# Modulation sums moved within a hybrid mLSTM / gated-delta-rule block, and a quarter of the feed-forward input scaled by GpSimd

## The chip, the cores and the metric

The kernel runs on one core of one Trainium2 chip. Five engines of the core matter here: TensorE (PE in the profile) multiplies matrices, VectorE (DVE), ScalarE (ACT) and GpSimd (POOL) work on elements, and SyncE (SP) issues most of the large loads. Each takes its own instructions in the order in which the program lists them. The metric is the device time of one launch in microseconds: the median of the runs of a kernel.

## The reference

One transformer-like layer on 256 tokens of width 2048, in fp32:

- `mod = silu(c) @ W_ada + b_ada`, cut into six rows of 2048: shift, scale and gate for the mixer and for the feed-forward part. In the kernel each 128 of its 12288 columns is one sum over a row of 2048 products: these are the **modulation sums**.
- `h = RMSNorm(x)*(1+scale_m)+shift_m`, then one input projection of `h`, whose columns feed an mLSTM branch (4 heads), a **gated delta rule** branch (16 heads of 128, chunks of 64, both directions) and two merge gates.
- Per chunk the delta rule needs the inverse of a unit-triangular 64x64 matrix, then `u = T(beta v)`, `w = T(beta e^g k)`, and a scan `S = a S + k^T v_new`; the output is normed per head and gated.
- Both branches are projected, merged and projected out ("o"), `x = x + gate_m * out`.
- `hf = RMSNorm(x)*(1+scale_f)+shift_f`, `x = x + gate_f * ((silu(hf W_gate) * (hf W_up)) W_down)`, and a last RMSNorm.

## The kernel before, in words

Weights arrive as fp32, 1 MB at a time on SP's queue (`raw`, 4 buffers). ScalarE rounds a half of such a piece to `wh` (L171, L197), VectorE makes the remainder `wl` (L172, L198), each with 3 buffers, and TensorE runs three passes: `wh` by the high and the low part of the activations, `wl` by the high part. A job of 4 pieces for two token tiles is `tjob` (L182-245; matmuls of 128x512 at L215, L216, L218), a job for a column block with the tokens as columns is `fjob` (L162-180; 128x256 at L175, L177). `acc_<job>` names the accumulators.

The **delta rule** goes in four groups g of four heads, each in two pairs p of two heads. Between groups the inverse of the blocks is begun on VectorE (`gdn_invert`, 30 steps of two operations at L663 and L669 on the tile `uu`), stored to memory by GpSimd (L655), read back in another layout as `cg` (L682), transposed and mixed into `R` (L684-689). Then `gdn_phase2` (L707-804) is a chain of short steps in which each engine waits for the other: `p1` (TensorE, L717) to `pt0` (VectorE, L718) to `p2` (L726) to `Et` and `X` (VectorE L729, ScalarE L730-733) to `p3` (L739) to `pt1` (L740) to `p4` (L751) to `UL` (L752, L753) to `pa` (L763, L764) to `z` (L767, L768) to `pb` (L775) to `r` (L776) to `pc` to `z` to `po` (L785-790) to a norm (`gdn_norm`, L805-822: squares on ScalarE at L809, a square root at L813, reciprocal L814, four scalings on VectorE at L819) to `px` (L796) and out (L798). The jobs of the other projections stand between these steps as **filler**: `stream` and `fill` put pieces of jobs there, by the tables `after` and `last`.

The **modulation sums** are one generator per part of 2048 columns (`ada_part`, L120-131). One sum is a 1 MB load on SP's queue and one VectorE operation on 128x2048 (L127), with the buffers of `raw` or, later, of the tile `ada`. Parts 2, 3 and 4 (48 sums) belong to the mixer's gate and the feed-forward's shift and scale; part 5 (16 sums) to the last gate. `sums(n)` runs the next n of them, and `pump()`, which every job calls after each of its pieces, runs one on each `every[0]`-th call; zero stops it. The output projection "o" has four quarters g (512 columns each), and calls `sums()` at the steps that a table names. After its last quarter come the residual (L1113, L1114), the token's norm (L1123-1125), the feed-forward input scaled by the norm (`normed`, into `xn`, L1191 or L1193), its transpose (`pxn`, L1200), scale and shift into `hf` (L1204 or L1206), the high and low parts (L1207, L1210), and the first gate job.

The order in which the instructions stand on each engine isn't the order of the Python text alone: the kernel is built with a scheduler that simulates the engines' time lines (`schedule_with_timeline_sim=True`), and places each operation where its simulation has it ready. Only operations inside `order(...)` keep the text's order among themselves. So an edit in one place can move rows in many.

Of the kernel before, what the change touches and what calls it, by code (L numbers as in the profile page):

```python
# [12 lines left out]
ALU = mybir.AluOpType  # L13
# [39 lines left out]
def hybrid_block(ctx: ExitStack, tc: tile.TileContext, xr, nfr, crow, pk_d, cst_d, ada2, ada4, win0, winb, wint, wba, wbb, wo, wgu, wd, out, dbg=None):  # L53
    nc = tc.nc
    V, S, G, PE = nc.vector, nc.scalar, nc.gpsimd, nc.tensor

    def pool(stack, name, bufs=1, **kw):
        return stack.enter_context(tc.tile_pool(name=name, bufs=bufs, **kw))
# [27 lines left out]
    def order(ins, yes=True):  # L86

        return tc.keep_in_program_order(ins) if yes else ins
# [58 lines left out]
    count, every = [0], [0]  # L147
# [97 lines left out]
    def run(job):  # L245
        for _ in job:
            pass
# [3 lines left out]
    def fill(n=1):  # L251

        while n and fills:
            if next(fills[0], None):
                n -= 1
            else:
                fills.pop(0)
# [633 lines left out]
    for g in range(4):  # L891
        if g == 3:
            sf.close()
            op = pool(so, "op", side="right")
        blocks = gdn_blocks(g)
        next(blocks)
        fill(8)
        next(blocks)
        fill(1)
        pairs = [gdn_phase2(g, p) for p in range(2)]  # L900
        every[0] = (0, 2, 2, 2)[g]
        for p in range(2):
            pieces = stream(4 * g + 2 * p + 4)
            if g == 3:
                o4s += [o_load(i, op, 3) for i in ((0, 1), (2,))[p]]
            for n in range(1, 10):
                next(pairs[p], None)
                if p == 0:
                    next(blocks, None)
                for _ in range(after[n] if g < 3 else last[n]):  # L910
                    next(pieces)
            for _ in pairs[p]:
                pass

            if g < 3:
                while 4 * g + 2 * p + 5 not in heads:
                    next(pieces)
        if g < 3:
            fills.insert(0, z_job(g + 1))
            every[0] = 0  # L920
            invert(g + 1)
# [166 lines left out]
    mgh, mgl = big(bigC, F32R, "mgh"), big(bigC, F32R, "mgl")  # L1088
    for g in range(4):
        if g == 3:  # L1090
            every[0] = 0
            while len(background) > 2:
                sums()
            row_store(2, ml, 0.5)
        run(y_a(g, mgh, mgl))
# [32 lines left out]
    rs1 = xp.tile([P, 3], F32, name="rs1")  # L1128
# [23 lines left out]
    for g in range(4):  # L1152
        def done_o(*a, g=g):
            for t, ps in [a] if g == 3 else enumerate(a[0]):
                residual(t, g, ps, gm, ss1, wp, g == 3)
                if g == 3:
                    token_rstd(ss1, rs1, t)

        if g == 3:
            root()  # L1160
        between = (lambda: next(gt0)) if g == 3 else None
        for i, _ in enumerate(tjob(f"o{g}", [wo[g, u] for u in range(4)], mgh, mgl, done_o, by_token=between)):
            if i in ((4, 6, 7), (1, 2, 4, 6), (1, 2, 4, 6), (1, 2, 4))[g]:
                sums()
            if g == 3 and i == 4:
                sums(P)
                V.scalar_tensor_tensor(
                    affn, mod[:, 4 * KB : 5 * KB], 1.0, pk[:, PK_NFFN : PK_NFFN + KB], ALU.add, ALU.mult
                )
# [16 lines left out]
    def normed(q, t, parts, eng):  # L1186
        if q not in xns:
            xns[q] = hp.tile([P, 2, 512], F32, tag="sg", bufs=2, name=f"xn{q}")
        o, i = xns[q][:, t, parts], x1[:, t, q * 512 + parts.start : q * 512 + parts.stop]
        if eng is V:  # L1190
            order(V.tensor_scalar(o, i, rs1[:, t : t + 1], None, ALU.mult))  # L1191
        else:
            order(S.activation(o, i, AF.Copy, scale=rs1[:, t : t + 1]))  # L1193

    def moved(b):

        px = gps(f"pxn{b}")
        for t in range(2):
            f = b % 4 * P
            order(PE.transpose(px[:, t * P : (t + 1) * P], xns[b // 4][:, t, f : f + P], ident))  # L1200
        hfs[b] = hp.tile([P, T], F32, tag="hf", bufs=2, name=f"hf{b}")
        f, m = affn[:, b : b + 1], mod[:, 3 * KB + b : 3 * KB + b + 1]
        if b % 2 and b > 2:
            order(S.activation(hfs[b], px[:, 0:T], AF.Identity, scale=f, bias=m))  # L1204
        else:
            order(V.tensor_scalar(hfs[b], px[:, 0:T], f, m, ALU.mult, ALU.add))  # L1206
        order(S.activation(hfh[:, b], hfs[b], AF.Copy))  # L1207
# [5 lines left out]
    normed(0, 1, slice(0, 256), V)  # L1213
    for t in range(2):
        normed(0, t, slice(256, 512), S)
    moved(0)
    moved(1)
    low(0)
# [4 lines left out]
    for b in range(2, KB, 2):  # L1223

        next(gt0)
        low(b)
        low(b + 1)
        next(gt0)
        if b % 4 == 2 and b < 12:
            for t in range(2):  # L1230
                normed(b // 4 + 1, t, slice(0, 512), S)
        for e in (b + 2, b + 3):
            if e < KB:
                moved(e)
# [3 lines left out]
    for j in range(FB // 4):  # L1238
# [4 lines left out]
        for e2 in range(2):  # L1243
# [5 lines left out]
            b = 4 * j + 2 * e2  # L1249
# [144 lines left out]
```

## Time and profile before

| what | value |
| --- | --- |
| median of 3 runs (lowest, highest) | 1985.31 us (1982.88, 1988.02) |
| the profiled execution: time, span | 1979.27 us, 1977.3 us |
| its mean granted TensorE clock | 0.988 |
| PE busy | 1918.9 us, 97% of the span |
| DVE / ACT / POOL busy | 1402.5 / 1022.7 / 96.9 us |
| the two chains of delta-rule group 3 | 861.69 to 948.23 us |
| from the last quarter of o into the first gate job | about 1250 to 1290 us |

Times in the trace are microseconds from the start of the span, and they are those of one execution, which took 6.0 us less than the median. A row of a time line gives start, length, engine, line, operation and tiles; what stands in brackets is how long the engine was idle before it and which operation it waited for. Matmul lengths overlap, since they are pipelined.

### The profile page before, as it was taken

To read this page: it belongs to the slowest core of one execution; us is meant where nothing else is said; L and a number is where in the kernel's file an instruction comes from. 1 tells how busy PE (TensorE), PEld (TensorE's weight loads), DVE (VectorE), ACT (ScalarE), POOL (GpSimd) and SP (SyncE) were. 2 spreads that over 40 slices of the span, in tenths; PEclk is the share of its full clock that TensorE was granted. 3 is DMA by queue.
4 is the path that set the end of the run, shared out by engine and by line. 5 is a ranking of instruction groups with operands and counts; after the bars stand their busy time and mean duration, and the time that the engine had idled before them with its cause. 6 is when DMAs were issued, how large, how long until landed. Compare 5 with 4: busy or idle time off the path is not lost.

```text
span 1977.3 us, 27036 instructions
## 1 busy us (share of the span) xinstructions
PE 1918.9 (97%) x10352; PEld 1705.5 (86%) x10352; DVE 1402.5 (71%) x2091; ACT 1022.7 (52%) x1568; POOL 96.9 (5%) x185
## 2 busy tenths in 40 slices
PE   8999999999999999999799999799999999999997
PEld 6887889989989998998688888688888888888886
DVE  5779887878988996965587769766666655555554
ACT  3146657855765686465454444554444444444443
POOL 0000300110100011000200000000000000000000
PEclk9999999999999999999799999899999999999999
DMA  9996665567667765885677679466766765566563
GB/s 400 420 383 194 222 223 192 167 203 283 228 199 247 281 214 191 310 303 190 234 291 266 249 288 419 182 234 235 265 244 237 262 246 193 205 240 203 202 206 114
DMA packets 78675, 487.76 MB, mean 247 GB/s; under 512 B 10265, under 2 KB 15681, under 8 KB 23889
## 3 DMA queue, kind: packets, MB, share of 16 engines
q1 hardware_dynamic: 63360, 450.95, 62.2%
q0 software_dynamic: 7872, 19.99, 4.4%
q10 hardware_dynamic: 7314, 15.10, 2.1%
q8 instruction: 81, 1.33, 0.3%
q14 instruction: 48, 0.39, 0.1%
HBM read 469.16 MB, written 16.83 MB: 246 GB/s over the span
## 4 chain that ended last, share of the span: by engine, by line
PE 73%; DVE 11%; DMA 9%; ACT 4%; issue 2%; POOL 0%; SPq 0%; ACTq 0%; DVEq 0%; POOLq 0%
DMA ra<-ada 5%; PE acc_up L215 4%; PE acc_up L218 4%; PE acc_up L216 4%; PE acc_d L216 4%; PE acc_d L215 4%; PE acc_d L218 4%; PE acc_gt L216 4%; PE acc_gt L215 4%; PE acc_gt L218 4%; PE acc_o L218 2%; PE acc_o L216 2%; PE acc_o L215 2%; PE acc_a L175 2%; PE acc_b L175 2%
## 5 line engine op out<-in xcount | busy, mean ns | idle before, releaser
L198 DVE TENSOR_TENSOR wl_d<-raw_d,wh_d 128x1024 fp32r<-128x1024 f32 x88 | 107.8, 1225 | 102.7 <-ACT wh_d L197 102.7
L127 DVE SCALAR_TENSOR_TENSOR ada<-ada,crow 128x2048 f32<-128x2048 f32 x64 | 146.5, 2289 | 43.6 <-DMA ada<-ada 43.5
L198 DVE TENSOR_TENSOR wl_up<-raw_up,wh_up 128x1024 fp32r<-128x1024 f32 x88 | 107.5, 1225 | 95.9 <-ACT wh_up L197 95.9
L197 ACT ACTIVATE wh_d<-raw_d 128x1024 fp32r<-128x1024 f32 x88 | 93.0, 1057 | 130.5 <-PE acc_d L216 125.3
L198 DVE TENSOR_TENSOR wl_gt<-raw_gt,wh_gt 128x1024 fp32r<-128x1024 f32 x88 | 107.7, 1224 | 72.4 <-ACT wh_gt L197 68.2
L197 ACT ACTIVATE wh_gt<-raw_gt 128x1024 fp32r<-128x1024 f32 x88 | 92.9, 1056 | 120.7 <-PE acc_gt L216 73.2
L197 ACT ACTIVATE wh_up<-raw_up 128x1024 fp32r<-128x1024 f32 x88 | 93.0, 1056 | 118.2 <-PE acc_up L216 71.7
L215 PE MATMUL acc_gt<-wh_gt,hfh 128*128 128x512 f32 x352 | 135.2, 384 | 0.0
L216 PE MATMUL acc_gt<-wh_gt,hfl 128*128 128x512 f32 x352 | 134.6, 382 | 0.0
L175 PE MATMUL acc_b<-hh,wh_b 128*128 128x256 f32 x576 | 134.6, 276 | 0.0
L175 PE MATMUL acc_b<-hl,wh_b 128*128 128x256 f32 x576 | 134.6, 277 | 0.0
L215 PE MATMUL acc_up<-wh_up,hfh 128*128 128x512 f32 x352 | 133.5, 379 | 0.0
L216 PE MATMUL acc_up<-wh_up,hfl 128*128 128x512 f32 x352 | 133.5, 379 | 0.0
L216 PE MATMUL acc_d<-wh_d,ffl 128*128 128x512 f32 x344 | 130.4, 379 | 0.0
L215 PE MATMUL acc_d<-wh_d,ffh 128*128 128x512 f32 x344 | 130.4, 379 | 0.0
L530 PE MATMUL first<-x,raw 128*128 128x256 f32 x512 | 114.5, 382 | 7.5 <-ACT x L523 6.8
L530 PEld LDWEIGHTS first<-x,raw 128*128 128x128 f32 x512 | 96.1, 190 | 25.9 <-ACT x L523 12.4
L175 PEld LDWEIGHTS acc_b<-hl,wh_b 128*128 128x128 f32 x576 | 110.6, 192 | 0.4
L175 PEld LDWEIGHTS acc_b<-hh,wh_b 128*128 128x128 f32 x576 | 110.5, 192 | 0.5
L197 ACT ACTIVATE wh_o<-raw_o 128x1024 fp32r<-128x1024 f32 x64 | 67.1, 1054 | 58.9 <-PE acc_o L216 35.5
L218 PE MATMUL acc_gt<-wl_gt,hfh 128*128 128x512 f32 x352 | 95.3, 385 | 0.0
L171 ACT ACTIVATE wh_b<-raw_b 128x1024 fp32r<-128x1024 f32 x72 | 76.1, 1058 | 37.1 <-PE acc_b L175 22.8
(384 smaller groups left out, 5018.4 us busy)
## 6 DMA issues: line engine op xcount, KB each, us to landing
ada<-ada SPq DMA_DIRECT2D x64, 1024.0 KB, 5.8
raw_gt<-wgu SPq DMA_DIRECT2D x44, 1024.0 KB, 5.0
raw_up<-wgu SPq DMA_DIRECT2D x44, 1024.0 KB, 4.9
raw_d<-wd SPq DMA_DIRECT2D x44, 1024.0 KB, 4.9
raw_b<-winb SPq DMA_DIRECT2D x36, 1024.0 KB, 5.0
ra<-ada SPq DMA_DIRECT2D x32, 1025.0 KB, 15.8
raw<-win SPq DMA_DIRECT2D x16, 1024.0 KB, 17.1
raw_z<-wint SPq DMA_DIRECT2D x16, 1024.0 KB, 5.2
```

Source lines behind the costliest of these rows:

```text
L127: V.scalar_tensor_tensor(raw, raw, 1.0, row_c[:, :D], ALU.mult, ALU.mult, accum_out=mod[:, c0 + b : c0 + b + 1])
L171: S.activation(wh, raw[:, k0 : k0 + 8], AF.Copy)
L175: PE.matmul(o, wh[:, k], both(x, k0 + k).rearrange("p a b -> p b a"), start=k0 + k + i == 0, stop=False)
L197: order(S.activation(wh, raws[u][:, k0 : k0 + 2], AF.Copy), hold)
L198: order(V.tensor_tensor(wl, raws[u][:, k0 : k0 + 2], wh.bitcast(F32), ALU.subtract), hold)
L215: order(PE.matmul(ps[t], tok(xh, kk, t), turns(wh[:, k]), start=kk == 0, stop=False), early and steps > 1)
L216: PE.matmul(ps[t], tok(xl, kk, t), turns(wh[:, k]), start=False, stop=False)
L218: PE.matmul(ps[t], tok(xh, kk, t), turns(wl[:, k]), start=False, stop=kk == last)
L530: PE.matmul(first[o], raw[:, o], x[:, b], start=b == 0 and o % 2 == 0, stop=b == KB - 1 and o % 2 == 1)
```

## The change

Four things, all outside the arithmetic:

1. In the delta rule's group 0, `every[0]` is 3 in place of 0: one modulation sum on each third `pump()` while its two chains and their filler run. Groups 1 to 3 keep 2.
2. Before the last quarter of the mLSTM branch's projection `y_a`, `every[0] = 0` is gone. The value stays 2 from there to the line `every[0] = 4` after the feed-forward input.
3. The table of o's own sums becomes `(4,6,7), (2,4,6), (1,3), ()`: none in its last quarter.
4. The second quarter of the feed-forward input (`normed(1, ...)`) goes to GpSimd, right after the first quarter, and the third and fourth, still on ScalarE, are asked for at blocks 4 and 8 in place of 6 and 10.

```diff
-        every[0] = (0, 2, 2, 2)[g]
+        every[0] = (3, 2, 2, 2)[g]
...
     for g in range(4):
         if g == 3:
-            every[0] = 0
             while len(background) > 2:
                 sums()
...
-            if i in ((4, 6, 7), (1, 2, 4, 6), (1, 2, 4, 6), (1, 2, 4))[g]:
+            if i in ((4, 6, 7), (2, 4, 6), (1, 3), ())[g]:
                 sums()
...
-        if eng is V:
-            order(V.tensor_scalar(o, i, rs1[:, t : t + 1], None, ALU.mult))
+        if eng is not S:
+            order(eng.tensor_scalar(o, i, rs1[:, t : t + 1], None, ALU.mult))
...
+    for t in range(2):
+        normed(1, t, slice(0, 512), G)
...
-        if b % 4 == 2 and b < 12:
+        if b % 4 == 0 and b < 12:
             for t in range(2):
                 normed(b // 4 + 1, t, slice(0, 512), S)
```

One line fewer from L1091 on makes the changed kernel's lines one smaller than before in the residual and the feed-forward input (L1112 there is L1113 here).

Where it moves instructions: first **TensorE in group 3's first chain**. `p_3_0` are the chain's small products, `acc_...` the accumulators of filler jobs (o and a are mLSTM projections, ma a merge gate). Before:

```order
L218 MATMUL acc_o_0_8664<-wl_o_3_2_8856,hh 128x512
L751 MATMUL p_3_0_8333<-X,pt_3_0_8303 128x64 x4
L218 MATMUL acc_o_1_8665<-wl_o_3_2_8856,hh 128x512
...
L175 MATMUL acc_a_0_8875<-hl,wh_a_0_0_8878 128x256
L177 MATMUL acc_a_0_8875<-hh,wl_a_0_0_8879 128x256 x2
L763 MATMUL pa_0_8383<-vv_6624,UL 128x128
L177 MATMUL acc_a_0_8875<-hh,wl_a_0_0_8879 128x256 x6
L764 MATMUL pa_0_8383<-vv_6624,UL 128x128
L763 MATMUL pa_0_8383<-vv_6864,UL 128x128
```

and with the change:

```order
L218 MATMUL acc_ma_0_9193<-wl_ma_3_2_9344,hh 128x512
L218 MATMUL acc_ma_1_9194<-wl_ma_3_2_9344,hh 128x512
L717 MATMUL p_3_0_8237<-R,cc_1107 128x32
L717 MATMUL p_3_0_8237<-R,cc_1108 128x32
...
L726 MATMUL p_3_0_8268<-R,pt_3_0_8238 128x32 x4
L739 MATMUL p_3_0_8320<-X,cc_1107 128x64
L739 MATMUL p_3_0_8320<-X,cc_1108 128x64
...
L751 MATMUL p_3_0_8351<-X,pt_3_0_8321 128x64 x4
L763 MATMUL pa_0_8401<-vv_6640,UL 128x128
L764 MATMUL pa_0_8401<-vv_6640,UL 128x128
```

Before, each step of the chain has matmuls of filler jobs ahead of it and behind it. Now the filler job `ma` ends before `p1` (L717), and from there to the last `px` (L796) of the second pair no row of an `acc_` tile stands on TensorE; the jobs o, a and ma all lie ahead of it.

Second, **VectorE at the same place** (`wl_...` are remainders of filler weights, `ada_...` modulation sums). Before:

```order
L718 TENSOR_TENSOR pt_3_0_8222<-p_3_0_8221,cst 128x512
L198 TENSOR_TENSOR wl_o_2_0_8758<-raw_o_2_8755,wh_o_2_0_8757 128x1024
L198 TENSOR_TENSOR wl_o_2_2_8781<-raw_o_2_8755,wh_o_2_2_8780 128x1024
L729 STREAM_TRANSPOSE Et_0_8257<-p_3_0_8252 128x128
L127 SCALAR_TENSOR_TENSOR ada_5_8934,mod<-ada_5_8934,crow 128x2048
L198 TENSOR_TENSOR wl_o_3_0_8811<-raw_o_3_8808,wh_o_3_0_8810 128x1024
L198 TENSOR_TENSOR wl_o_3_2_8856<-raw_o_3_8808,wh_o_3_2_8855 128x1024
L740 TENSOR_TENSOR pt_3_0_8303<-p_3_0_8302,cst 128x512
L172 TENSOR_TENSOR wl_a_0_0_8879<-raw_a_0_8876,wh_a_0_0_8878 128x1024
```

With the change:

```order
L198 TENSOR_TENSOR wl_yb_0_0_9389<-raw_yb_0_9386,wh_yb_0_0_9388 128x1024
L198 TENSOR_TENSOR wl_yb_0_2_9405<-raw_yb_0_9386,wh_yb_0_2_9404 128x1024
L127 SCALAR_TENSOR_TENSOR ada_13_9523,mod<-ada_13_9523,crow 128x2048
L684 STREAM_TRANSPOSE cg_7955<-cg_7955 128x512
L688 TENSOR_SCALAR R<-cg_7955,cst 128x256
L689 SCALAR_TENSOR_TENSOR R<-cg_7955,cst,R 128x256
L688 TENSOR_SCALAR R<-cg_7955,cst 128x256
L689 SCALAR_TENSOR_TENSOR R<-cg_7955,cst,R 128x256
L718 TENSOR_TENSOR pt_3_0_8238<-p_3_0_8237,cst 128x512
L729 STREAM_TRANSPOSE Et_0_8273<-p_3_0_8268 128x128
L740 TENSOR_TENSOR pt_3_0_8321<-p_3_0_8320,cst 128x512
```

The chain's rows `pt`, `Et`, `pt`, ... now follow each other directly, with the transposes and mixes of `cg` and `R` right before, and two remainders for the next job (`yb`) and a sum ahead of those.

Group 1's second pair is in part alike: no filler job stands there between `pa` and `px`. Between the chains more filler stands than before: from the second pair's `px` of group 0 to group 1's `p1`, and from that of group 1 to group 2's `p1`.

Third, **VectorE at the end of o** (`tmss` is the residual's product of token tile 0 or 1, `rs` the norm). Before:

```order
L198 TENSOR_TENSOR wl_gt_0_0_11570<-raw_gt_0_11567,wh_gt_0_0_11569 128x1024
L1113 TENSOR_TENSOR tmss_10970_0_3_11585<-acc_o_0_11445,gm 128x512
L127 SCALAR_TENSOR_TENSOR ada_14_11481,mod<-ada_14_11481,crow 128x2048
L1114 TENSOR_TENSOR x_10966<-x_10966,tmss_10970_0_3_11585 128x512
L1123 TENSOR_REDUCE rs_10971<-ss_10970 128x1
L1125 RECIPROCAL rs_10971<-rs_10971 128x1
L1113 TENSOR_TENSOR tmss_10970_1_3_11604<-acc_o_1_11446,gm 128x512
L1114 TENSOR_TENSOR x_10966<-x_10966,tmss_10970_1_3_11604 128x512
L127 SCALAR_TENSOR_TENSOR ada_15_11502,mod<-ada_15_11502,crow 128x2048
L1123 TENSOR_REDUCE rs_10971<-ss_10970 128x1
```

With the change:

```order
L198 TENSOR_TENSOR wl_gt_0_0_11570<-raw_gt_0_11567,wh_gt_0_0_11569 128x1024
L1112 TENSOR_TENSOR tmss_10994_0_3_11585<-acc_o_0_11452,gm 128x512
L127 SCALAR_TENSOR_TENSOR ada_0_11777,mod<-ada_0_11777,crow 128x2048
L1113 TENSOR_TENSOR x_10990<-x_10990,tmss_10994_0_3_11585 128x512
L1122 TENSOR_REDUCE rs_10995<-ss_10994 128x1
L1124 RECIPROCAL rs_10995<-rs_10995 128x1
L1112 TENSOR_TENSOR tmss_10994_1_3_11604<-acc_o_1_11453,gm 128x512
...
L1209 TENSOR_TENSOR hfl<-hf_11697,hfh 128x256
L127 SCALAR_TENSOR_TENSOR ada_1_11889,mod<-ada_1_11889,crow 128x2048
L198 TENSOR_TENSOR wl_gt_1_2_11715<-raw_gt_1_11682,wh_gt_1_2_11714 128x1024
```

One sum still stands between the product and the addition of token tile 0's residual. It is now the first of part 5, since `pump()` runs while the first gate job's pieces are made, and a second one of part 5 stands between the gate's remainders. The sum behind token tile 1's residual is gone. On GpSimd two TENSOR_SCALAR rows (128x512, `xn`) stand where nothing stood, with one ISA row ahead of them. Over the whole program the 48 sums of parts 2 to 4 are all done in the first quarter of o, at the latest.

## The prediction

> **What bounds the kernel now.** I read the engine shares first, then the busy time by stretches, then what TensorE waits for, and last the time lines of three places.
>
> ```profile
> span 1977.3 us, 27036 instructions
> PE 1918.9 (97%) x10352; PEld 1705.5 (86%) x10352; DVE 1402.5 (71%) x2091; ACT 1022.7 (52%) x1568; POOL 96.9 (5%) x185
> ```
>
> TensorE is busy 1918.9 of 1977.3 us; all idle time in the whole program is 58.4 us. The change adds and removes no matmul, so the time can only move with TensorE's idle time and its granted clock. Stretches (the engines' busy time in each):
>
> ```profile
> core 0: us, PE busy (x) PEld busy (x) DVE busy (x) ACT busy (x) POOL busy (x), PEclk, DMA share, GB/s
> 300.00:350.00 50.00, 49.05 (x396) 47.59 (x395) 39.77 (x82) 39.61 (x81) 3.84 (x7) 1.00 0.52 181
> 550.00:600.00 50.00, 47.09 (x301) 42.76 (x300) 39.78 (x90) 33.95 (x72) 6.93 (x14) 1.00 0.68 202
> 861.69:948.23 86.54, 79.66 (x536) 73.61 (x534) 45.25 (x58) 49.60 (x101) 0.00 (x0) 0.99 0.64 229
> 1250.00:1300.00 50.00, 38.35 (x174) 31.55 (x173) 31.64 (x52) 28.47 (x51) 0.00 (x0) 0.90 0.35 121
> ```
>
> In 1250 to 1300, where o ends and the feed-forward input is made, TensorE idles 11.65 us. In 861.69 to 948.23, group 3's two delta-rule chains, it idles only 6.88 us, because filler lies between the steps:
>
> ```profile
> L175 PE MATMUL acc_a<-hl,wh_a 128*128 128x256 f32 x64 | 15.5, 283 | 0.0
> ...
> L216 PE MATMUL acc_ma<-wh_ma,hl 128*128 128x512 f32 x32 | 12.3, 384 | 0.0
> ...
> L218 PE MATMUL acc_o<-wl_o,hh 128*128 128x512 f32 x28 | 7.4, 382 | 0.0
> L775 PE MATMUL pb<-z,gg 128*128 128x128 f32 x16 | 2.5, 280 | 2.3 <-DVE r L776 2.3
> L796 PE MATMUL px<-cst,on 128*128 128x128 f32 x8 | 2.4, 370 | 3.9 <-DVE on L819 3.3 <-ACT obt L798 0.6
> L786 PE MATMUL po<-z,at 128*128 128x128 f32 x8 | 1.6, 288 | 0.7 <-ACT z L768 0.7
> ```
>
> Nine such groups of `acc_a`, `acc_ma` and `acc_o` hold most of the window's 536 matmuls, all with no idle time before them; the idle time stands before `pb`, `po` and `px`, the last steps of the second chain, where the filler had run out. So this trace already holds one piece of bare chain, and its price.
>
> **The change part by part.**
>
> *Group 3's chains without filler.* The order of TensorE's rows has no accumulating row from `p1` of the first pair to the last `px` of the second. TensorE takes its rows in order, so each hop to VectorE or ScalarE is now idle time. The hops, by the second chain of before:
>
> ```profile
> 909.29 0.69 DVE L718 TENSOR_TENSOR pt<-p,cst 128x512 f32<-128x512 f32 x1 [0.65 <-PE p L717]
> ...
> 914.65 0.32 DVE L729 STREAM_TRANSPOSE Et<-p 128x128 f32<-128x128 f32 x1 [0.16 <-PE p L726]
> ...
> 923.61 0.69 DVE L740 TENSOR_TENSOR pt<-p,cst 128x512 f32<-128x512 f32 x1
> ...
> 928.10 0.43 DVE L753 COPY UL<-p 64x256 f32<-64x256 f32 x1 [1.31 <-ACT UL L752]
> ...
> 938.28 0.42 DVE L776 TENSOR_TENSOR r<-vv,pb 128x256 f32<-128x256 f32 x1 [0.87 <-PE pb L775]
> ```
>
> ```profile
> 915.00 0.27 ACT L730 ACTIVATE X<-p 32x128 f32<-32x128 f32 x1 [1.47 <-DVE Et L729]
> ...
> 915.88 0.30 ACT L733 ACTIVATE X<-Et 32x128 f32<-32x128 f32 x1
> ...
> 933.17 0.37 ACT L767 ACTIVATE z<-pa,sm 128x128 f32<-128x128 f32 x1 [1.56 <-PE pa L764]
> ...
> 933.93 0.38 ACT L768 ACTIVATE z<-pa,sm 128x128 f32<-128x128 f32 x1
> ...
> 944.10 1.28 ACT L813 ACT_TABLE_LOAD   x1
> ```
>
> From `p1` to `p2` 0.69 us; from `p2` to `p3` the transpose and four copies, 914.65 to 916.18 or 1.53; `p3` to `p4` 0.69; `p4` to `pa` 0.43; `pa` to `pb` the four `z`, 933.17 to 934.31 or 1.14; from `pb` to `pc` one `r` of 0.42; `pc` to `po` 0.71 as measured above; `po` to `px` 3.34 as measured (four squares, a table load of 1.28 us and a square root, a reciprocal, four scalings). That is 8.9 us, and about 0.1 us for each of eight hand-overs makes 9.7 us a pair. Two pairs idle 19.4; before pays 6.88 there already. Difference **+12.5 us**. Lower end +9 (no hand-over cost, and `px` partly under the next pair's `p1`), upper end +17 (`pb` takes its measured 2.3 in both pairs).
>
> *The stall before the first chain.* `p1` needs `R`, and `R` comes from the inverse by way of memory:
>
> ```profile
> 844.05 0.17 DVE L669 TENSOR_TENSOR uu<-uu,utmp 64x30 f32<-64x30 f32 x1
> ...
> 857.03 0.71 DVE L684 STREAM_TRANSPOSE cg<-cg 128x512 f32<-128x512 f32 x1 [2.54 <-DMA cg<-inv_d]
> ...
> 859.81 0.48 DVE L689 SCALAR_TENSOR_TENSOR R<-cg,cst,R 128x256 f32<-128x256 f32 x1
> ```
>
> ```profile
> 861.26 0.38 PE L216 MATMUL acc_o<-wh_o,hl 128*128 128x512 f32 x1
> 861.47 0.38 PE L215 MATMUL acc_o<-wh_o,hh 128*128 128x512 f32 x1
> 861.69 0.97 PE L717 MATMUL p<-R,cc 128*128 128x32 f32 x8
> ```
>
> From the inverse's last operation to `R` it is 860.29 less 844.22, 16.1 us. Before, TensorE did filler for all of it. With the change the last filler remainder, `wl_ma_3_2`, stands five small rows ahead of the inverse's end, so TensorE has only what it lags behind VectorE: up to three remainder buffers of 12 matmuls each. One such half piece takes 2.6 us (the spacing of `acc_o` rows, 0.215, times 12), so the lag is 2.6 to 7.8 us. One sum and two `yb` remainders also stand ahead of `cg`'s transpose, but its load is later than they. 16.1 less 7.8 is +8.3: I take **+8**, from +3 (load path a third quicker with less traffic) to +13.
>
> *Group 1's second pair.* From `pa` to `px` it is bare: 1.14 + 0.4 + 0.7 + 3.3, 5.5 us; a few head products stand between. **+5**, 2 to 6.
>
> *The clock.* The granted clock falls to half in spells:
>
> ```profile
> 945.99:956.23 10.24, 5.84 (x14) 3.70 (x15) 4.47 (x7) 3.90 (x5) 4.85 (x8) 0.50 0.48 158
> ...
> 966.47:980.12 13.65, 13.16 (x44) 11.36 (x43) 7.23 (x19) 6.21 (x10) 2.03 (x4) 0.50 0.47 158
> 1256.60:1263.43 6.83, 2.92 (x11) 2.45 (x12) 5.98 (x14) 3.11 (x9) 0.00 (x0) 0.50 0.00 0
> ...
> 1277.08:1280.49 3.41, 3.41 (x10) 2.66 (x9) 1.93 (x4) 2.23 (x4) 0.00 (x0) 0.50 0.00 0
> ```
>
> The first of them follows the bare end of the second chain with its 3.34 us before `px`; four spells make 34.1 us, 8.5 us each. With the change there are three more such places: the wait for `R`, the first chain's `px`, and the `px` of group 1's second pair. Three spells of 8.5 us, TensorE busy half of each, and half of that work lost: 3 x 8.5 x 0.5 x 0.5 = **+6**; from 0 (the clock holds) to +15 (half clock through the whole bare stretch of some 50 us: there are about 168 small matmuls at 0.11 to 0.15 us, near 20 us of work, which would take 15 to 20 us more, partly in place of waits).
>
> The Trainium skill's "TensorE: Matmul & The Clock Gate" ("Why this matters for your kernels") says that idle gaps between bursts over about 3 us bring the clock back to half, and shorter ones don't. The row 945.99:956.23 agrees, behind idle times of 3.34 us. By that rule the bare hops of 0.4 to 1.5 us are harmless and the term stays by the three long gaps; if the measure were the busy share, the +15 would apply.
>
> *What it saves.* Filler that stands elsewhere can close the small gaps of groups 0 to 2; the rows 300:350 and 550:600 show 0.95 and 2.91 us of them. **-2**, 0 to -4.
>
> *The end of o.*
>
> ```profile
> PE pxn L1200 <- ACT xn L1193: 11.6, 7, 6.8
> ```
>
> ```profile
> 1251.77 2.28 DVE L127 SCALAR_TENSOR_TENSOR ada<-ada,crow 128x2048 f32<-128x2048 f32 x1
> ...
> 1257.37 2.28 DVE L127 SCALAR_TENSOR_TENSOR ada<-ada,crow 128x2048 f32<-128x2048 f32 x1
> ...
> 1268.22 0.54 DVE L1206 TENSOR_SCALAR hf<-pxn,affn,mod 128x256 f32<-128x256 f32 x1 [0.39 <-PE pxn L1200]
> ...
> 1272.24 0.54 DVE L1206 TENSOR_SCALAR hf<-pxn,affn,mod 128x256 f32<-128x256 f32 x1
> ```
>
> All that the change aims at here is 11.6 us of waiting for `xn`, of which 6.8 is the first. Of the two sums of 2.28 us that delay the norm, one goes, but token tile 0's still has one, of part 5, whose load is asked for late (behind the gate's second piece). The first `xn` comes about 0.7 us earlier, since only token 1's addition was behind the second sum. The three later waits, 4.8 us with their second halves, end at GpSimd's `xn` and at the earlier ones; but two blocks of input take VectorE and ScalarE 4.02 us (1268.22 to 1272.24) against TensorE's 12 matmuls of 0.215, 2.6, plus transposes, so most of these waits come back as waits for `hf`. And part 5's second sum (2.28) goes into that same loop. **-1.5**, from -6 to +2. GpSimd is idle in this window (POOL 0.00 in the row 1250 to 1300), and no such operation of GpSimd is in the trace; two of 128x512 at anything up to 3 us each are done before block 4's transposes, 6.7 us after the first.
>
> By the Trainium skill's "GPSIMD Engine Reference" (2.1), the first call of a freshly loaded GpSimd routine pays about 6 us. An ISA row stands ahead of the two; if it loads then, the second quarter would come some 1 us late, and the sum would be -0.5 there. No row of before can show it.
>
> *The sum.* 12.5 + 8 + 5 + 6 - 2 - 1.5 = +28 us. The profiled execution's 1979.27 becomes 2007.3; since it ran 6.0 us under the median, I give the forecast on the median: 1985.31 + 28 = **2013 us**. The six sums that go into group 0 cost nothing by themselves: at 2.28 us each (the rows of L127 above) they are under 14 us of VectorE, which had 10 us free in each of the 50 us of the rows 300:350 and 550:600, and TensorE's filler covers them. Without that cover each would cost what the chain then waits, up to 2.28 us.
>
> **The rivals.** *No stall, steady clock*: TensorE lags by a full ring and the load path is short, and the clock stays at 1.0: 12.5 + 3 + 5 + 0 - 3.5 = +17, 2002 us. For it: nearly all of the bare waits are short. Against it: the half clock from 945.99. *Half clock over the whole bare stretch, slow load path*: 14 + 10 + 6 + 15 - 2 = +43, 2028 us. For it: the row 966.47:980.12, half clock with TensorE busy 13.16 of 13.65 us, so a spell can last beyond its gap. *The gain at the end of o outweighs the chains* (faster): `xn` from GpSimd and the earlier requests end all 11.6 us of waits there, the clock there (0.90 over 50 us, some 3 us of work) comes back, and the small gaps (4) go: -18.6. The chains cost less than the bounds above, 9 in all, since the second chain starts before the first one's `px`: 1976 us. It decides only if VectorE's loop per two blocks falls under TensorE's 3.2 (against 4.02 here), and the order lets the pairs overlap, which the first `px` row ahead of the second pair's `p1` speaks against. *No change*: filler that was done earlier lets TensorE finish as early at `px`, since the chain starts sooner by as much as it lost; a start some 25 us sooner than the filler alone allows would take back the whole sum: 1985. Against it: the wait of 16.1 us for `R` begins where the inverse ends, and VectorE has the same filler remainders ahead of that end.
>
> **How the numbers follow.** Forecast (2006 to 2020) 0.45; no stall, steady clock (1992 to 2006) 0.25; half clock, slow load (2020 to 2040) 0.17; no change 0.07; faster 0.06. Range 1992 to 2033: it leaves out the faster case, no change and a part of the upper end. A measurement of this kernel tells 0.3%, 6 us, from no change; by the cases faster 0.06, same 0.07, slower 0.87.
>
> **What would show it.** Right: no `acc_` row between the first `p1` and the last `px` of group 3, TensorE busy under half in that stretch of 45 to 55 us, waits of L726, L739, L751, L764, L775 and L786 on their VectorE and ScalarE hops in the list of waits, L717's wait for `R` of 3 to 13 us, PEclk under 1.0 near 900. Wrong: a group-3 stretch with little idle time, or `pxn`'s waits gone together with those for `hf`, or a new long wait elsewhere that carries more than these.

## The result and the profile after

The changed kernel takes 2045.48 us (median of 4 runs, 2044.13 to 2049.47) against 1986.66 us of the kernel before beside it (1982.88 to 1988.71): a ratio of 1.0302, 95% interval 1.0279 to 1.0325, 58.8 us slower. The direction was as forecast, the size was twice it: 2013 us, and 1992 to 2033 as range.

The page of the changed kernel (span, busy time, and the granted clock by fortieths of the span):

```profile
span 2044.7 us, 27044 instructions
...
PE 1944.1 (95%) x10352; PEld 1722.8 (84%) x10352; DVE 1399.2 (68%) x2091; ACT 1027.1 (50%) x1568; POOL 100.6 (5%) x187
...
PEclk9999999999999999997689999999999999999999
```

The span grew by 67.4 us. TensorE's busy time grew by 25.2 us though it does the same 10352 matmuls, so a part of the loss isn't waiting but slower work: the tenths of the granted clock show 7, 6 and 8 from 920 to 1073 us. What TensorE waits for (us in total, times, longest):

```profile
PE p L717 <- DVE R L689: 10.9, 2, 10.1
...
PE px L796 <- DVE on L819: 6.9, 3, 3.3
PE pxn L1199 <- ACT xn L1192: 6.4, 1, 6.4
PE acc_mb L215 <- ACT ev_ma L332: 5.2, 2, 3.0
...
PE acc_o L215 <- ACT ev_mb L332: 5.0, 1, 5.0
PE acc_gt L215 <- ACT hfh L1206: 4.1, 4, 2.9
PE acc_ya L218 <- DVE wl_ya L198: 4.0, 3, 1.8
...
PE p L739 <- ACT X L733: 3.2, 2, 1.6
```

The first row is new and is the forecast stall: `p1` waits for `R`, 10.1 us at once. `p L739 <- ACT X` is the hop from `p2` to `p3`, which filler covered before. The rows `ev_ma` and `ev_mb` (an accumulator that ScalarE hasn't emptied) are new as well, and `wl_ya` grew from 0.5 us; these were not forecast.

Stretches of the changed kernel (window, length, then busy us and count by engine, granted clock, DMA share, GB/s): group 3's two chains up to the next job, and the end of o:

```profile
955.57:1015.24 59.67, 38.38 (x169) 34.03 (x169) 9.90 (x29) 22.61 (x74) 0.48 (x1) 0.59 0.03 10
1320.00:1370.00 50.00, 39.51 (x181) 31.89 (x180) 35.32 (x53) 29.30 (x50) 3.29 (x2) 0.93 0.48 171
```

From the first `p1` of group 3 to the next job it is 59.7 us, with TensorE busy 38.4 us at a mean clock of 0.59. Before, 861.69 to 951.77 held the same chain steps and nearly all of the jobs o, a and ma, at a mean clock of 0.97.

By place, with the time between the same rows in both traces: up to the first `yb` matmul +63.5 us (951.77 to 1015.24), the mLSTM part +0.2 (124.4 and 124.6), `y_a` +5.1 (92.8 and 97.9), o +0.2, from o's last matmul to the first `up` matmul -1.5 (38.2 and 36.7), the rest 0. Of the 63.5, TensorE's idle time is 37.5: 10.1 before the chain, 17.8 less 6.9 or 11.0 within it, and 16.5 before group 3. The other 26 are a longer busy time for the same matmuls. Most of that is the clock: up to the first `yb` matmul TensorE was busy 49.4 us at half clock, and 4.8 before. At half clock the spacing of matmuls of `acc_o` is twice as long (0.43 us at 877.82, 0.215 at 882.33), so half of the difference, some 22 us, is an estimate of the clock's part: 16 from group 3's `p1` to the next job, and 6 ahead of it. What the last 4 are isn't settled.

### The profile page after: what moved, and what is told of

Same layout as the page of the kernel before. It is cut to its first block, busy times and chain, and to the rows that moved or that the text cites. A ratio compares the mean times of both kernels' runs of the same rounds, so it can differ in the third digit from the quotient of the medians.

```text
span 2044.7 us, 27044 instructions
## 1 busy us (share of the span) xinstructions
PE 1944.1 (95%) x10352; PEld 1722.8 (84%) x10352; DVE 1399.2 (68%) x2091; ACT 1027.1 (50%) x1568; POOL 100.6 (5%) x187
## 4 chain that ended last, share of the span: by engine, by line
PE 74%; DMA 10%; DVE 8%; ACT 5%; issue 3%; POOL 0%; ACTq 0%; SPq 0%; DVEq 0%; POOLq 0%
PE acc_b L175 6%; DMA ra<-ada 4%; PE acc_up L216 4%; PE acc_up L218 4%; PE acc_up L215 4%; PE acc_d L215 4%; PE acc_d L216 4%; PE acc_d L218 4%; PE acc_gt L216 3%; PE acc_gt L215 3%; PE acc_gt L218 3%; DMA ada<-ada 3%; PE acc_b L177 3%; PE acc_o L218 2%; PE acc_o L215 2%
## 5 line engine op out<-in xcount | busy, mean ns | idle before, releaser
L198 DVE TENSOR_TENSOR wl_up<-raw_up,wh_up 128x1024 fp32r<-128x1024 f32 x88 | 107.6, 1224 | 100.1 <-ACT wh_up L197 100.1
L171 ACT ACTIVATE wh_b<-raw_b 128x1024 fp32r<-128x1024 f32 x72 | 76.1, 1058 | 61.7 <-PE acc_b L175 36.7
L198 DVE TENSOR_TENSOR wl_o<-raw_o,wh_o 128x1024 fp32r<-128x1024 f32 x64 | 77.1, 1218 | 30.2 <-ACT wh_o L197 30.2
```

Of the source, the lines that this page charges most:

```text
L171: S.activation(wh, raw[:, k0 : k0 + 8], AF.Copy)
L198: order(V.tensor_tensor(wl, raws[u][:, k0 : k0 + 2], wh.bitcast(F32), ALU.subtract), hold)
```

## The experiments

The first theory was that group 0's number alone makes the loss, by way of the order of the filler; its rivals were the other edits, and the sums' own work.

**Group 0 back at 0, all other edits kept.**

```diff
-        every[0] = (3, 2, 2, 2)[g]
+        every[0] = (0, 2, 2, 2)[g]
```

> The changed kernel with every[0] back at 0 in group 0; the other edits (part 5's sums from y_a's last quarter on, o's table, GpSimd's quarter) stay. The filler of group 3 stands between the chain's steps as before. Theory (group 0's number alone makes the loss, by the order of the filler): the loss of 59 us goes; left are the -1.6 us at the end of o and between 0 and +5 us of waits for sums in y_a: 1983 to 1990 us. Rival (the sums that later edits place in y_a, o and the first gate job carry a large part of the loss): 2005 us or more.

Measured: 1983.53 us, ratio to the kernel before 0.9988 (0.9974 to 1.0002). The loss is gone, and so is any gain. `y_a` takes 96.0 us in place of 92.8; from o's last matmul to `up` it is 35.0 in place of 38.2. The two cancel.

**Group 0's number alone.**

```diff
-        every[0] = (0, 2, 2, 2)[g]
+        every[0] = (3, 2, 2, 2)[g]
```

> The kernel before with every[0] = 3 in group 0 and nothing else. Theory: group 3's chains are bare, the clock falls there, the wait for R is 10 us: 2040 to 2050 us. Rival (a large part comes from the later edits): 2015 us or less.

Measured: 2043.07 us, 1.0281 (1.0256 to 1.0305). By the ratios, one number in one group brings 56 us of the change's 60, nearly the whole loss.

**The feed-forward input's edits alone** (GpSimd for the second quarter, requests at blocks 4 and 8).

```diff
+    for t in range(2):
+        normed(1, t, slice(0, 512), G)
...
-        if b % 4 == 2 and b < 12:
+        if b % 4 == 0 and b < 12:
```

> The kernel before with the feed-forward input's edits alone (second quarter on GpSimd, third and fourth asked for at blocks 4 and 8); all sums stay where they were. Theory: the waits of pxn at 1267, 1275 and 1284 go, most of them come back as waits for hf: -1 to -4 us, 1982 to 1985 us. Rival (hidden anyway, the loop over blocks bounds it): 0.

Measured: 1980.20 us, 0.9974 (0.9960 to 0.9988), a little below the expected range. From 1250 to 1300 us its waits are

```profile
PE pxn L1200 <- ACT xn L1193: 6.9, 1, 6.9
PE acc_gt L215 <- ACT hfh L1207: 1.3, 3, 0.4
```

so of 11.6 us in seven waits only the first, 6.9, is left, and 1.3 us come back as waits for `hfh`. The waits for `xn` go as the edits intend; the gain is small, and its interval leaves out 1.

**Eight in place of three in group 0.**

```diff
-        every[0] = (3, 2, 2, 2)[g]
+        every[0] = (8, 2, 2, 2)[g]
```

> The changed kernel with 8 in place of 3 in group 0: two sums there instead of six. By its order group 3's chains are just as bare, but the second pair of group 1 has filler from pa to px. Theory: 5 to 12 us less than the change, 2033 to 2041 us. Rival (the number of sums in group 0 sets the loss): a third of it, about 2005 us.

Measured: 2038.67 us, 1.0266 (1.0246 to 1.0285), as the first theory expected. With two sums in group 0 the loss is nearly what it is with six; it doesn't go by their number.

**All matmuls of the pairs held in the text's order.**

```diff
+        pin[0] = g in (0, 1, 2, 3)      # each matmul of the pairs' loop: keep program order
         for p in range(2):
             pieces = stream(4 * g + 2 * p + 4)
```

> The changed kernel with all matmuls of the four groups' pairs held in the order of the program's text, so that filler can't be moved ahead of the chains; the sums of group 0 and all other edits stay. Theory (the place of the filler is what costs): 1983 to 1998 us, the chains of group 3 hidden, clock 1.0 there. Rival (the six sums in group 0, their loads and 2.3 us each of VectorE, cost the time themselves): over 2020 us.

Measured: 2122.34 us, 1.0690 (1.0658 to 1.0722). Neither theory is tested by it, since the strict order has waits of its own (L61 and L65 are lines of the wrapper through which the matmuls and transposes go):

```profile
PE p L61 <- DVE R L702: 34.3, 3, 12.7
PE vps L65 <- ACT vf L332: 24.9, 8, 5.8
...
PE pb L61 <- DVE r L789: 18.4, 8, 4.6
```

`p1` waits in each group: 34.3 us for `R` in three of them, and 18.5 us in the first, where the profile names no releaser. The heads' products (`vps`) stand where their inputs are late. In the changed kernel the scheduler has moved matmuls past most of these waits.

**Held in group 3 only**, with 12 half pieces of filler ahead of `p1` there.

```diff
-        fill(8)
+        fill(8 if g < 3 else 12)
...
+        pin[0] = g in (3,)    # chain matmuls and the first matmul of each filler half piece
```

> The changed kernel with group 3's chain matmuls and the first matmul of each filler half piece there held in the order of the program's text, and 12 pieces of filler ahead of p1 there; group 0's sums and all other edits stay. Group 3's pairs have 34 and 33 us of filler between their steps again; the second pairs of groups 1 and 2 still lack it from pa to px. Theory (the filler's place makes the loss, not the sums in group 0): group 3's 37.5 us of idle time and half clock there go, some 10 us come back in group 2: 2000 to 2017 us. Rival (the sums cost it): 2035 us or more.

Measured: 2037.51 us, 1.0267 (1.0239 to 1.0295), which is where the rival put it. `p1` now waits 39.4 us for `R` in one piece (up to 891.52 us), and TensorE stands idle through it (busy 0.02 of 39.4 us). The filler was held inside the chain, and so it was missing ahead of it. That turned the question round: not where group 3's filler stands, but why `R` of group 3 is so late against TensorE's stock of filler.

**What the traces say of that.** The inverse of group 1 on VectorE runs from 424.6 to 464.5 us before, and from 458.3 to 552.1 with the change. VectorE's groups in that stretch of the kernel before (busy us, mean ns, idle before):

```profile
L198 DVE TENSOR_TENSOR wl_mb<-raw_mb,wh_mb 128x1024 fp32r<-128x1024 f32 x8 | 9.7, 1209 | 0.0
...
L663 DVE TENSOR_TENSOR utmp<-uu 64x30 f32<-64x30 f32 (+14 forms) x30 | 9.6, 321 | 3.6 <-issue 2.8
L198 DVE TENSOR_TENSOR wl_ma<-raw_ma,wh_ma 128x1024 fp32r<-128x1024 f32 x4 | 4.8, 1210 | 0.0
L198 DVE TENSOR_TENSOR wl_o<-raw_o,wh_o 128x1024 fp32r<-128x1024 f32 x2 | 2.4, 1210 | 0.0
L172 DVE TENSOR_TENSOR wl_b<-raw_b,wh_b 128x1024 fp32r<-128x1024 f32 x2 | 2.4, 1207 | 0.0
L127 DVE SCALAR_TENSOR_TENSOR ada<-ada,crow 128x2048 f32<-128x2048 f32 x1 | 2.3, 2294 | 0.0
```

and of the changed one:

```profile
L172 DVE TENSOR_TENSOR wl_b<-raw_b,wh_b 128x1024 fp32r<-128x1024 f32 x24 | 28.9, 1207 | 0.0
L127 DVE SCALAR_TENSOR_TENSOR ada<-ada,crow 128x2048 f32<-128x2048 f32 x8 | 18.3, 2282 | 1.8 <-DMA ada<-ada 1.8
L318 DVE SCALAR_TENSOR_TENSOR cv<-pad,pk,cv 128x256 f32<-128x256 f32 x40 | 18.2, 468 | 0.0
L198 DVE TENSOR_TENSOR wl_o<-raw_o,wh_o 128x1024 fp32r<-128x1024 f32 x8 | 9.7, 1211 | 0.2 <-ACT wh_o L197 0.2
...
L663 DVE TENSOR_TENSOR utmp<-uu 64x30 f32<-64x30 f32 (+14 forms) x30 | 9.5, 317 | 0.3
L172 DVE TENSOR_TENSOR wl_a<-raw_a,wh_a 128x1024 fp32r<-128x1024 f32 x2 | 2.4, 1206 | 0.0
```

The inverse's own work is the same (L663 x30). But 16 filler remainders and one sum stood among its steps before; now it is 35 remainders, 8 sums and 40 rows `cv` (a convolution that prepares the heads). In the traces the four inverses hold 15, 16, 17 and 19 remainders before, and 21, 35, 29 and 16 with the change. They take 38.0, 39.9, 40.8 and 50.1 us before, and 56.3, 93.8, 75.9 and 39.8 after. Each is about 2.6 us times its remainders (39, 42, 44, 49, and 55, 91, 75, 42), which is the time of a filler half piece on TensorE, and TensorE is busy throughout, so no wait shows there, but the filler is spent. VectorE is just as full, though: it is busy 38.4 of 39.9 us in group 1's inverse before, and 90.8 of 93.8 with the change, where sums and `cv` take 36.5 of them. So these rows don't tell whether the filler on TensorE or all that stands in VectorE's order sets the pace. An inverse with no remainder at all, in the kernel with group 3 held, took 21.4 us, and those with 9 in the kernels below 31 to 37. From group 0's `p1` to group 1's it was 166 us and is 232; the later groups keep their distance (182 and 197 before, 193 and 193 after). By group 3 the filler is gone. The second theory was that stretched inverses use up the filler, and that the sums themselves cost little.

**An inverse stretched with no sum in group 0.** In a kernel without group 0's sums, and with none from o's last quarter on, filler is held in the text's order in the inverses, 8 half pieces ahead. One kernel has one half piece at each step's break, the other 4 and 3 in groups 1 and 2.

```diff
-        fill(4)
+        fill(8)
+        pin[0] = True      # high parts and remainders: keep program order
         for _ in gen:
-            fill(1)
+            fill((1, 4, 3, 1)[g])
+        pin[0] = False
```

> The same with group 0 at 0 and no sums from o's last quarter on. What is left between this and the run above is what the sums of group 0, y_a and the first gate job cost under one order of the filler. Theory: 6 to 12 us less than the run above, 1978 to 2000 us. Rival: 25 us less or more.

> The kernel of the run above (no sum in group 0), but with 4 and 3 filler half pieces between the inverse's steps of groups 1 and 2 in place of 1: 36 and 27 remainders there by the order, as the change has 35 and 29, and group 3's chains without filler. Theory: an inverse takes 2.6 us for each remainder, 94 and 70 us; group 3 is bare as with the change, and the kernel loses as much without any sum in group 0: 2035 to 2065 us. Rival (it needs the sums): 2010 us or less.

Measured: 2032.43 us (1.0242, 1.0226 to 1.0258) with 9 remainders in each inverse, and 2118.20 us (1.0670, 1.0647 to 1.0693) with 36 and 27 in groups 1 and 2. The second lies above its range, 86 us over the first, with no sum in group 0. In the profiled executions 62 us of 77 come up to the first `yb` matmul. Another 17 come at the end of o, where TensorE waits 15.6 us for `hfh`: six sums are still undone there and stand on VectorE ahead of `hf`, from 1380.50 to 1396.46 us. So stretching two inverses is enough to empty group 3, and at most the 62 are the price of that. The two inverses took 107.6 and 76.6 us (3.0 and 2.8 us for a remainder), with VectorE busy only 61.0 and 50.1 us of it, so here the filler paced them, with waits for ScalarE's high parts, and not VectorE's own work. `p1` of group 3 then waits 38.6 us:

```profile
PE p L718 <- DVE R L690: 38.6, 1, 38.6
```

The first of the two is itself 48 us slower than the kernel before, though it was expected at 2000 us at most. Its inverses are short, 33 to 37 us, and it pays for that:

```profile
PE acc_v L219 <- DVE wl_v L199: 10.3, 2, 9.8
PE acc_mb L216 <- ACT wh_mb L198: 7.3, 3, 2.5
...
PE acc_ma L216 <- ACT wh_ma L198: 5.8, 3, 2.0
```

Holding the order of the filler on VectorE and ScalarE makes TensorE wait for `wl_v` and for high parts. These rows hold some 23 us. Up to the first `yb` matmul TensorE is also busy 31.2 us at half clock in place of 4.8, which costs some 13 by the same estimate as above. The rest was not settled.

**The sums' own cost, under that same order.** The change's sums and edits, with the hold and 8 half pieces:

```diff
-        fill(4)
+        fill(8)
+        pin[0] = True
```

> As the changed kernel with the filler held in the inverses, but with 8 half pieces ahead of the hold in place of 4, so that the wait for the inverse's load doesn't stand ahead of remainders that TensorE needs. Theory (stretched inverses make the loss): the waits of v and z for their remainders go, inverses under 40 us: 1985 to 2010 us. Rival (the sums in group 0 delay the chains themselves): 2030 us or more.

Measured: 2040.08 us, 1.0285 (1.0268 to 1.0303), which is where the rival put it. What speaks against the rival is the kernel beside it: without group 0's sums (and without sums in o's last quarter and the first gate job) it took 2032.43 us, only 7.7 less. An earlier pair of the same kind, with 4 half pieces ahead of the hold, had a wait of its own:

> The changed kernel, all its edits and group 0's sums kept, with the filler's high parts and remainders held in the order of the program's text while an inverse runs, so that 9 remainders stand between an inverse's steps in place of 20, 35, 29 and 16 (before: 15 to 18). By the order, all eight chains then have filler between their steps. Theory now (group 0's number lets the scheduler put more filler into the inverses of groups 0 to 2, which stretches them and uses up the filler that group 3 needs; the sums themselves cost little): the inverses take under 50 us each, group 3's idle time is at most what it was before, 1975 to 1992 us. Rival (the sums in group 0 and their loads themselves delay the heads and chains): 2010 us or more.

> The same hold in the kernel with group 0 at 0 and no sums from o's last quarter on (the input's edits, part 5 not in the first gate job). Theory: the hold keeps filler for group 3's last steps, where before 6.9 us of idle time and 24 us of half clock lie: 1968 to 1978 us, under the 1978 us without the hold. Rival (the last chain's end is bare whatever the filler, or the inverse then waits elsewhere): 1976 to 1985 us.

Measured: 2056.57 us (1.0362, 1.0333 to 1.0391) and 2032.60 (1.0251, 1.0228 to 1.0274). The first is where its rival put it, the second is above both of its ranges. In the second, VectorE stands idle 6.2 us before the inverse's first step, which reads the loaded tile `uu` (the profile names no releaser), with filler remainders queued behind it, and TensorE waits for them (`psc` is a product of the mLSTM part that waits for a load):

```profile
PE acc_z L219 <- DVE wl_z L199: 19.3, 5, 6.7
PE acc_v L219 <- DVE wl_v L199: 16.1, 2, 14.8
PE psc L960 <- DMA mkq<-kq_d: 9.2, 1, 9.2
```

This pair puts the sums at 24 us, the other at 8. Their own cost under one order of the filler isn't settled, since a hold has waits of its own in which a part of it can hide. In neither pair is it half of the 59 us.

**The clock.** Extra matmuls, whose results nobody reads, were put into group 3's bare chains to keep TensorE busy in the waits.

```diff
+        warm(4, p2[:, 256:512], pt0[:, 3], R[:, 1])     # 4 matmuls of 128x256 behind p2; 2 behind p1, p3, p4
...
+        warm(10, px[:, 0:256], hd[1][2][:, 1, P:256], z[:, 1, 2:4])
```

> The changed kernel with 20 extra matmuls of 128x256 in each of group 3's two chains, where TensorE waits (2 behind p1, 4 behind p2, 2 behind p3, 2 behind p4, 10 ahead of px), into unused columns; their results aren't read, and no other row moves. Theory (a large part of the bare chains' loss is the clock, which a waiting TensorE lets fall to half): the clock comes back to 1.0 for most of the stretch from p1 to the next job, which falls from 59.7 us to 42 to 50; the kernel to 2028 to 2037 us. Rival (the loss is the waits alone, the clock is a symptom): no gain, 2045 us or more.

Measured: 2061.12 us, 1.0381 (1.0360 to 1.0402). That is in the rival's range. The clock did come back for the second pair, but the pair got no shorter (26.84 us here, 26.75 in the changed kernel); its two pairs are

```profile
959.78:997.69 37.91, 31.46 (x120) 26.11 (x121) 5.29 (x15) 13.37 (x42) 0.00 (x0) 0.60 0.00 0
997.69:1024.53 26.84, 21.27 (x129) 17.27 (x127) 4.60 (x13) 7.64 (x29) 0.00 (x0) 1.00 0.03 10
```

The wait for `X` still follows the extra matmuls in full (1.62 us before L745): they wrote into the tile that VectorE and ScalarE read, and so these waited for them. In the second form they write into the tile that is free until `px`:

```diff
+        px = gps(f"px_{g}_{p}")      # at the start of the pair, in group 3
...
+        warm(3, pt0[:, 3], R[:, 1])  # into px[:, 0:256]; 2 behind p3, 2 behind p4, 7 ahead of px
```

> The changed kernel with 14 extra matmuls of 128x256 in each of group 3's chains, written into the tile that is free until px, so that no other engine waits for them (before, the extra matmuls wrote into tiles that VectorE waited for, and lengthened the chain by their own time). Their results are overwritten. Theory (half clock costs about 10 us a pair): the second pair runs at clock 1.0 and takes 19 to 22 us from p1 to px in place of 26.8; the kernel 2030 to 2041 us. Rival (the waits alone): pairs no shorter, 2045 us or more.

Measured: 2041.80 us, 1.0289 (1.0259 to 1.0319), 0.8 us above the expected range.

```profile
958.46:1008.94 50.48, 41.27 (x225) 36.61 (x225) 9.81 (x29) 22.61 (x74) 0.48 (x1) 0.83 0.04 12
```

With work added, the stretch from `p1` to the next job is 50.5 us in place of 59.7, at clock 0.83 in place of 0.59. The second pair's `p1` also stands earlier in the order here, so a part of the 9 us is overlap. One stretch is free of that: from the second pair's `p2` to the end of its wait for `z` before `po` the chain has the same steps in the same order. In the changed kernel it is the first row, here the second:

```profile
988.21:1005.22 17.01, 12.36 (x51) 10.99 (x50) 2.28 (x5) 4.89 (x17) 0.00 (x0) 0.51 0.05 15
986.41:998.53 12.12, 10.21 (x70) 8.91 (x68) 3.36 (x10) 5.37 (x18) 0.00 (x0) 1.00 0.07 23
```

It is 4.9 us shorter at clock 1.00 than at 0.51, though it holds extra matmuls. So the clock lengthens the chain and isn't only a symptom of the waits. For the kernel that isn't shown: only 3.5 us are left in the span (`p1` came 2.9 later and the mLSTM part took 3.0 more), and the ratios, 1.0289 here and 1.0302 for the change, overlap in their intervals.

**A version that beats both.** Group 0 at 0, the input's edits, the sums of `y_a` kept on, and none from o's last quarter to the first gate job's end.

```diff
-        every[0] = (3, 2, 2, 2)[g]
+        every[0] = (0, 2, 2, 2)[g]
...
         if g == 3:
+            every[0] = 0
             root()
```

> The changed kernel with group 0 at 0, and every[0] = 0 from o's last quarter on, so that the 48 sums are done before o's last quarter and none of part 5 runs in the first gate job. Theory: the first xn comes some 3 us earlier than with the input's edits alone, y_a's last quarter pays about 3 us for its sums: 1976 to 1982 us. Rival (the norm's chain has other waits as long): 1980 to 1984 us, no better than the input's edits alone.

Measured: 1978.19 us, 0.9959 (0.9944 to 0.9974): 7 us faster than the kernel before, 67 faster than the change. Its interval overlaps that of the input's edits alone, so a gain over those isn't shown. The end of o has

```profile
PE pxn L1200 <- ACT xn L1193: 3.5, 1, 3.5
PE acc_gt L215 <- ACT hfh L1207: 0.8, 2, 0.4
```

where before had 11.6 us, and `y_a` takes 96.6 us in place of 92.8 for the sums it now carries.

## Why the prediction was right or wrong

The direction and most of the places came out as forecast. Two steps failed in size, the clock and what the moved filler saves, and one term, the sums in `y_a`, was left out.

- *Filler gone from group 3, and the chains' idle time*: right. Forecast +12.5, measured +11.0; the first pair's waits are 0.8, 1.6, 0.9, 0.5, 0.9, 0.5, 0.6, 0.7 and 3.3 us, as the hops of before gave them. The sign "TensorE busy under half" there did not come: it was busy 38.4 of 59.7 us, since half clock lengthens its work.
- *The stall before `p1`*: right. Forecast +8, measured 10.1. The kernel with a stretched inverse and the one with group 3's filler held show that this wait grows to 39 us when the filler ahead of it goes.
- *Group 1's second pair*: forecast +5. From `pa` to `px` it waits 3.9 us (1.3 before `pc`, 1.3 before `px`, 0.5, 0.5 and 0.3), where before had 1.8, so +2.1; the heads' products stand between `po` and `px`.
- *The clock*: this is **the step that failed** by the most. It was sized +6; TensorE's busy time grew by 26, some 22 of it at half clock by the estimate above. I counted one spell after each of three long waits and took the short hops as harmless. In the changed kernel the spells lasted 30.7 and 20.5 us, through the short hops, and the bare stretch alone cost some 16. That is the price that the upper end, +15, and the rival "half clock over the whole bare stretch" had for it; the rival's 2028 us is too low by the next two terms and by some 6 us of half clock ahead of group 3.
- *What it saves*: **this step failed** too. Forecast -2; in truth there were 14 us more of waits before group 3 (16.5 less the 2.1 above). Accumulators that ScalarE had not emptied make 5.2 and 5.0 us, a remainder of o 2.0, the rest are waits before `p1` and `pa`. The 5.0 has this chain: a sum whose load was late kept VectorE, then ScalarE's square root and a table load of 1.28 us came late, then the emptying of `mb`. I took "filler stands elsewhere" as only good; with sums and remainders crowded into fewer places, VectorE's queue was the new wait in this case.
- *The sums that the removed line lets run in `y_a`*: I did not price this edit, and `y_a` took 5.1 us more. Not all of that is the edit's: with group 0's number alone, where the line stays, `y_a` takes 95.8 us, 3.0 more than before. Without group 0's sums it is 96.0, and 93.5 where the line stays (the input's edits alone), so the edit costs some 2.5.
- *The end of o*: forecast -1.5, measured -1.5, by luck. Of the 11.6 us, 6.4 is left as the first wait, and 4.1 came back as waits for `hfh`. The kernel with group 0's number alone, with none of these edits, is shorter still there, 34.8 us in its trace, so something other than these edits moves this place by as much. Without group 0's sums, part 5's sums cost 4 us there: 35.0 us with them, 31.2 in the version that beats both. In the change the 48 sums are done at 1277 us, in o's second quarter and not in its first.
- *The cause that I did not look for*: I read that rows had moved, and counted how much filler lay where, but not that the inverse of group 1 held 35 remainders in place of 16. That count was to be had from the order before any run. That a stretched inverse is enough to empty group 3 is shown; that it is all of the change's loss isn't, and the sums' own cost lies at 8 or 24 us. Why the scheduler puts the remainders there isn't shown by any run: group 1's inverse holds 35 with six sums in group 0 and 29 with two.

## What to carry to other kernels

An edit that only adds work to a slack engine can re-sort a scheduled program. Compare the orders, and count what stands within each latency chain as well as ahead of it: a chain's length goes with what its neighbours put among its steps, and filler that covers one chain is missing at the last. When a covered chain becomes bare, price it with half clock over the whole bare stretch (here 49 of 60 us), and not only by its waits. Test moved edits one at a time: here one number cost 56 us, and beside the other moved sums the input's edits no longer showed the 5 us that they gain alone.

## What the runs showed of the hardware

The granted clock has memory in a way that I had not expected. At full clock a window of 3.41 us with TensorE busy 47% kept 1.0 (935.74 us before, followed by another at 1.0), and windows busy 10% and 56% were followed by half clock:

```profile
935.74:939.16 3.42, 1.60 (x13) 1.60 (x14) 2.06 (x5) 0.96 (x2) 0.00 (x0) 1.00 0.67 160
942.57:945.99 3.42, 0.33 (x3) 0.14 (x2) 0.65 (x4) 2.63 (x10) 0.00 (x0) 1.00 0.54 228
```

The first two are of the kernel before, these of the changed one:

```profile
650.02:653.43 3.41, 1.91 (x16) 1.55 (x15) 2.91 (x17) 2.97 (x6) 1.55 (x4) 1.00 0.44 59
653.43:656.84 3.41, 3.41 (x19) 3.41 (x18) 2.26 (x10) 3.06 (x5) 0.00 (x0) 0.50 0.42 85
957.22:960.63 3.41, 2.18 (x10) 1.91 (x9) 1.01 (x2) 0.06 (x1) 0.00 (x0) 0.50 0.00 0
974.28:977.70 3.42, 2.70 (x13) 2.41 (x12) 0.07 (x1) 1.14 (x4) 0.00 (x0) 0.50 0.00 0
977.70:981.11 3.41, 3.41 (x18) 3.41 (x17) 0.00 (x0) 0.00 (x0) 0.00 (x0) 0.50 0.00 0
981.11:984.52 3.41, 0.42 (x4) 0.23 (x2) 0.55 (x4) 2.63 (x10) 0.00 (x0) 1.00 0.00 0
1001.59:1005.00 3.41, 2.92 (x14) 2.62 (x13) 0.42 (x1) 0.46 (x2) 0.00 (x0) 0.50 0.00 0
```

At half clock, windows busy 64% and 79% stayed at half; one busy throughout and one busy 86% were followed by 1.0. At half clock the chain keeps TensorE busy longer, and in most windows still not long enough: the clock was at half for 49 of the 60 us here. The Trainium skill's "TensorE: Matmul & The Clock Gate" ("Why this matters for your kernels") warns of idle gaps over about 3 us between bursts. In the changed kernel six of the nine falls follow gaps of 3.0 to 10.1 us and agree. Three don't: those at 339.40, 653.43 and 1011.83 us follow no gap over 2.3 us (1.3 at 653.43). The traces show besides that gaps of 0.5 to 1.6 us are enough to keep the clock down. A threshold of the busy share isn't settled by these rows, and the share alone doesn't decide: 47% held once and 56% didn't, and in the kernel before a window busy throughout (2.73 us of it products of 128x1 into `pden`) was followed by half clock, and one busy throughout at half clock stayed there:

```profile
1051.81:1055.21 3.40, 3.40 (x29) 3.32 (x28) 3.40 (x4) 1.10 (x3) 0.00 (x0) 1.00 0.92 316
966.47:969.88 3.41, 3.41 (x16) 3.15 (x14) 2.50 (x6) 1.90 (x2) 0.97 (x2) 0.50 1.00 365
```

GpSimd's two operations on 128x512 took 1.57 and 1.73 us (from 1326.05 us), under the 3 us each that the prediction allowed, and the first began as soon as its scale `rs` was there. The Trainium skill's "GPSIMD Engine Reference" (2.1) tells of some 6 us for the first call of a freshly loaded routine; no such time shows between `rs` and the operation in this trace or in that of the input's edits alone. Whether a load ran earlier, while GpSimd was idle, these rows don't show.
